# The mixer's two attentions as one pipeline of head pairs between projections

## The chip, the cores and the metric

The kernel runs on one core of a Trainium2 chip. The metric is device time of one execution in microseconds (us). The kernel before the change took 2604.03 us, the median of three runs (2603.2 to 2607.58).

## The reference, cut to what matters

Two transformer blocks follow each other on 256 tokens of width 1024, each two layers deep, all in float32. The change touches only the mixer sublayer of the first block, which runs twice (once in each layer):

```python
def mixer_sublayer(x, w_in, b_gate, kv_g, w_uk, w_uv, conv_w, w_branch, w_out, rel_bias):
    (qa, ckv, iq, ik, iw, qs, ks, vs, cb, cc, ch, ga, gb, gc) = jnp.split(x @ w_in, offsets, axis=-1)
    ckv = rms_norm(ckv, kv_g)
    y_a = dsa_branch(qa, ckv, iq, ik, iw, w_uk, w_uv, rel_bias)   # 8 heads, top-64 keys, softmax
    y_b = stick_breaking_branch(qs, ks, vs)                       # 8 heads of 64
    y_c = short_conv_branch(cb, cc, ch, conv_w)
    merged = (sigmoid(ga + b_gate[0]) * (y_a @ w_branch[0])
              + sigmoid(gb + b_gate[1]) * (y_b @ w_branch[1])
              + sigmoid(gc + b_gate[2]) * (y_c @ w_branch[2]))
    return merged @ w_out
```

`dsa_branch` scores all keys with eight index heads, keeps the best 64 of each query, and attends to a shared latent of width 128. `stick_breaking_branch` weighs key s by sig(z_ts) times the product of 1 - sig(z_tj) over the keys j between s and t.

## The kernel before, in words

Tokens lie in two blocks of 128. Every projection is a product of a weight and the activations, both split in two float32r parts, and takes three matmuls for each 128 rows of depth (`mm3`, L239 to L243). A projection of 2 x 128 output channels (`pair`, L252) is 48 such matmuls of 256 columns into one PSUM bank of the tag `pj`. Its weight comes in two halves of 512 KB through three buffers `wf` (SP issues the DMAs); ACT casts each half to `wh` (L236), DVE subtracts to get `wl` (L237). `wh` and `wl` have six buffers each. Everything else on TensorE, above all the attentions, uses plain float32 operands in the banks of the tag `pa`, four of them as well; a plain float32 matmul appears in the trace as two records.

The program is written in one order, but a scheduler arranges each engine's instructions within it, so projections written later are moved between the pieces of an attention.

In `mixer` the order as written is: the values `vs`; latent, index key and index weights; the index queries; eight index heads (L583 to L593: two score matmuls, a Relu on ACT, two accumulations on DVE each); the top-64 selection on DVE (L595 to L601); the projection `qa` (96 matmuls); the eight latent heads; the projections `qs` and `ks` (192); the eight stick heads; the short convolution (288); then for each of eight output blocks j its three gates (576 in all) and its branch product (36 each, 288 in all).

The heads run through `skew` (L209), a software pipeline: at step t the first stage works on unit t, the second on unit t - 1, and so on. A unit is one head. For the latent attention the stages are `logits` (every second head: the queries of a pair into the latent space, L626 and L627; a bias sum on GpSimd, L630 and L631; scores, L633 and L634; softmax), `turned` (three transposes, L316, copied out by ACT, L766), `latent` (L771, L772) and `values` (L656, into the left or right 64 columns of a bank). For the stick heads they are `sticks` (L675, L676, then sigmoids on ACT and scans on DVE), `turned` and `broken` (L771 and L772 with 64 output channels).

Side work is a generator queue: `fill(place)` advances it by the digits of the table `FILL` at the top of the file. In `logits` it takes three steps at the first three heads of each layer. Each step is a piece of the second block's modulation (L924: four matmuls on a tile `wa` of 512 KB, which has two buffers). `until(n)` (L229) forces the queue forward where its result is needed; the first place is the last feed-forward of the first block.

Of the kernel before, what the change touches and what calls it, by code (L numbers as in the profile page):

```python
# [13 lines left out]
AF = mybir.ActivationFunctionType  # L14
# [5 lines left out]
P = 128  # L20
# [94 lines left out]
class Net:  # L115
# [411 lines left out]
    def mixer(self, l, xs):  # L527
# [56 lines left out]
        for h in range(8):  # L584
            b = slice(64 * (h % 2), 64 * (h % 2) + 64)
            ps = self.ps()
            mm(ps[:, 0:P], iqT[b, h // 2, 0:P], ikT[b, 0:P], start=True, stop=True)
            mm(ps[:, P:384], iqT[b, h // 2, P:T], ikT[b, :], start=True, stop=True)
            re = self.a2()[:, :384]
            A.activation(re, ps[:, :384], AF.Relu)  # L590
            for tb, (a, e) in enumerate(G):
                prev = self.masks[:, 0, a:e] if h == 0 else sc[:, a:e]
                V.scalar_tensor_tensor(sc[:, a:e], re[:, a:e], iw[:, tb, h:h + 1], prev, ALU.mult, ALU.add)  # L593
# [22 lines left out]
        ys = [Split(self, 4) for _ in range(3)]  # L616
        qls, pos = {}, {}

        def logits(h, _):
            hp, i = divmod(h, 2)  # L620
            if i == 0:
                qls[hp] = self.a2().rearrange("p (c t) -> p c t", c=2)
                for j in range(2):
                    b = slice(64 * j, 64 * j + 64)
                    ps = self.ps()
                    mm(ps[:, :T], wuk[b, hp], qaT[b, hp], start=True, stop=True)  # L626
                    A.mul(qls[hp][:, j], ps[:, :T], 0.125)  # L627
            ql = qls[hp]
            bm = self.a2()[:, :384]
            nc.gpsimd.tensor_tensor(bm[:, P:384], t5[h // 4][:, h % 4, ::-1], sel[:, P:384], ALU.add)  # L630
            nc.gpsimd.tensor_tensor(bm[:, 0:P], t5[h // 4][:, h % 4, P - 1::-1], sel[:, 0:P], ALU.add)  # L631
            ps = self.ps()
            mm(ps[:, 0:P], ql[:, i, 0:P], ckT[:, 0:P], start=True, stop=True)  # L633
            mm(ps[:, P:384], ql[:, i, P:T], ckT, start=True, stop=True)  # L634
            V.tensor_tensor(bm, ps[:, :384], bm, ALU.add)
            p = self.a2()
            sm = self.softmax(bm, G, 1.0, p)
            self.scale_groups(p, G, sm)
            self.fill(f"logits{l}")
            return p  # L640

        def turned(h, p):
            return self.causalT(p)

        def latent(h, pT):
            ps = self.ps()
            self.causal_pv(ps[:, :T], [ckN[:, 0], ckN[:, 1]], pT)
            ol = self.a1()
            A.copy(ol, ps[:, :T])
            return ol  # L650

        def values(h, ol):
            hp, i = divmod(h, 2)
            if i == 0:
                pos[hp] = self.ps()
            mm(pos[hp][64 * i:64 * i + 64, :T], wuv[:, h], ol, start=True, stop=True)  # L656
            if i == 1:
                self.split(ys[0].h(hp), ys[0].l(hp), pos[hp][:, :T])

        self.skew([(h,) for h in range(8)], logits, turned, latent, values)  # L660


# [6 lines left out]
        pos = {}  # L669

# [22 lines left out]
        def broken(h, pT):  # L693
            hp, i = divmod(h, 2)
            if i == 0:
                pos[hp] = self.ps()
# [951 lines left out]
```

## Time and profile before

| | |
|---|---|
| median of the runs | 2604.03 us |
| the profiled execution | 2600.67 us |
| its span (first to last instruction) | 2598.8 us |
| TensorE busy | 2534.4 us (98%) |
| VectorE (DVE) busy | 1479.2 us (57%) |
| ScalarE (ACT) busy | 1175.3 us (45%) |
| GpSimd (POOL) busy | 66.7 us (3%) |
| read from HBM | 417.33 MB, 162 GB/s over the span |

Matmuls are pipelined: a row's duration is longer than the distance to the next row's start. What a matmul costs TensorE is therefore read from the difference of two starts. Idle time of an engine is told with what ended it.

### The profile page before, as it was taken

How to read it: one execution, taken by the hardware profiler on the slowest of the kernel's cores; microseconds unless marked ns; L12 is line 12 of the kernel's file. 1: busy time of each engine (PE TensorE's matmuls, PEld its weight loads, DVE VectorE, ACT ScalarE, POOL GpSimd, SP SyncE). 2: the span in 40 equal slices, each digit the busy share in tenths (PEclk: the TensorE clock that was granted, in tenths of full speed). 3: DMA queues.
4: the chain of work that ended last, by engine and by line, in shares of the span. 5: the costliest groups of instructions: out<-in, count | busy, mean ns of one | idle time of the engine just before them, and what ended most of it. 6: DMA issues, size and time to landing. Idle time of an engine off the chain costs nothing.

```text
span 2598.8 us, 40393 instructions
## 1 busy us (share of the span) xinstructions
PE 2534.4 (98%) x15946; PEld 2156.3 (83%) x15946; DVE 1479.2 (57%) x2974; ACT 1175.3 (45%) x1957; POOL 66.7 (3%) x88
## 2 busy tenths in 40 slices
PE   8999999999999999999999999899999999999999
PEld 7997889968988988799789877577888787777997
DVE  5556765556446547665665756776322337646644
ACT  5444454544444445544544545554222224445542
POOL 0000100000000000200000000000000000032000
PEclk9999999999999999999999999999999999999999
DMA  7565435655555555345665651434322434543553
GB/s 261 190 212 195 142 102 180 217 199 187 183 200 196 183 198 188 117 143 183 221 218 190 210 172 65 151 119 145 115 97 97 170 100 137 176 93 72 179 189 135
DMA packets 136493, 424.19 MB, mean 163 GB/s; under 512 B 29752, under 2 KB 32480, under 8 KB 136304
## 3 DMA queue, kind: packets, MB, share of 16 engines
q1 hardware_dynamic: 136304, 421.62, 49.3%
q8 instruction: 125, 2.05, 0.3%
q14 instruction: 64, 0.52, 0.1%
HBM read 417.33 MB, written 4.24 MB: 162 GB/s over the span
## 4 chain that ended last, share of the span: by engine, by line
PE 43%; DVE 3%; DMA 2%; ACT 1%; issue 1%; POOL 0%; SPq 0%; POOLq 0%; ACTq 0%; DVEq 0%
PE pj L241 8%; PE pj L242 8%; PE pj L243 8%; PE pa L242 4%; PE pa L241 4%; PE pa L243 4%; PE pa L316 2%; PE pj L924 1%; DMA wa<-in_mod_wB_dram 1%; DMA k<-in_rpbF_dram 1%; PE pj L1280 1%; DMA wf<-in_ffn_w_inA_dram 0%; PE pa L1295 0%; PE pj L1379 0%; PE pj L1243 0%
## 5 line engine op out<-in xcount | busy, mean ns | idle before, releaser
L237 DVE TENSOR_TENSOR wl<-wf,wh 128x1024 fp32r<-128x1024 f32 (+1 forms) x652 | 784.7, 1204 | 737.4 <-ACT wh L236 730.1
L236 ACT CAST wh<-wf 128x1024 fp32r<-128x1024 f32 (+1 forms) x652 | 670.7, 1032 | 930.8 <-PE pj L242 422.2
L241 PE MATMUL pj<-k,wh 128*128 128x256 f32 (+2 forms) x2896 | 840.6, 290 | 3.5 <-ACT k L236 3.5
L243 PE MATMUL pj<-k,wl 128*128 128x256 f32 (+2 forms) x2896 | 838.9, 290 | 0.0
L242 PE MATMUL pj<-k,wh 128*128 128x256 f32 (+2 forms) x2896 | 838.9, 290 | 0.0
L241 PEld LDWEIGHTS pj<-k,wh 128*128 128x128 f32 (+1 forms) x2896 | 554.2, 191 | 18.6 <-issue 6.6
L243 PEld LDWEIGHTS pj<-k,wl 128*128 128x128 f32 (+1 forms) x2896 | 554.1, 191 | 10.8 <-issue 3.4
L242 PEld LDWEIGHTS pj<-k,wh 128*128 128x128 f32 (+1 forms) x2896 | 554.0, 191 | 10.3 <-issue 3.2
L242 PE MATMUL pa<-wl,k 128*128 128x512 f32 x688 | 273.9, 398 | 0.0
L241 PE MATMUL pa<-wh,k 128*128 128x512 f32 x688 | 272.0, 395 | 0.0
L241 PE MATMUL pj<-wh,k 128*128 128x512 f32 (+1 forms) x616 | 246.9, 402 | 11.7 <-ACT wh L236 6.6
L242 PE MATMUL pj<-wl,k 128*128 128x512 f32 (+1 forms) x616 | 246.0, 400 | 0.0
L243 PE MATMUL pa<-wh,a 128*128 128x512 f32 x560 | 218.1, 389 | 0.0
L243 PE MATMUL pj<-wh,k 128*128 128x512 f32 (+1 forms) x496 | 197.4, 399 | 0.3 <-DVE k L237 0.3
L241 PEld LDWEIGHTS pa<-wh,k 128*128 128x128 f32 x688 | 128.8, 187 | 33.8 <-ACT wh L236 0.4
L241 PEld LDWEIGHTS pj<-wh,k 128*128 128x128 f32 x616 | 116.5, 189 | 48.3 <-issue 7.9
L242 PEld LDWEIGHTS pa<-wl,k 128*128 128x128 f32 x688 | 129.2, 188 | 28.4 <-issue 0.8
L242 PEld LDWEIGHTS pj<-wl,k 128*128 128x128 f32 x616 | 116.8, 190 | 29.7 <-DVE wl L237 2.3
L236 ACT CAST k<-k 128x512 fp32r<-128x512 f32 (+2 forms) x152 | 85.6, 578 | 104.2 <-PE pa L242 40.2
L243 PEld LDWEIGHTS pa<-wh,a 128*128 128x128 f32 x560 | 105.3, 188 | 25.3 <-issue 0.4
L243 PEld LDWEIGHTS pj<-wh,k 128*128 128x128 f32 x496 | 94.1, 190 | 23.3 <-DVE k L237 2.4
L316 PEld LDWEIGHTS pa<-ident,k 128*128 128x128 f32 x580 | 65.3, 143 | 50.3 <-issue 18.9
(254 smaller groups left out, 2461.7 us busy)
## 6 DMA issues: line engine op xcount, KB each, us to landing
wf<-in_ffn_w_inA_dram SPq DMA_DIRECT2D x262, 512.0 KB, 3.7
wf<-in_ffn_w_outB_dram SPq DMA_DIRECT2D x132, 512.0 KB, 3.9
wf<-in_mix_A_dram SPq DMA_DIRECT2D x108, 512.0 KB, 3.7
wa<-in_mod_wB_dram SPq DMA_DIRECT2D x96, 512.0 KB, 4.4
wf<-in_w_branchA_dram SPq DMA_DIRECT2D x32, 384.0 KB, 3.1
wf<-in_od_w_dram SPq DMA_DIRECT2D x24, 512.0 KB, 5.1
wf<-in_w_mix_outB_dram SPq DMA_DIRECT2D x16, 512.0 KB, 4.8
wf<-in_w_outB_dram SPq DMA_DIRECT2D x16, 512.0 KB, 7.9
```

The source lines that it names most:

```text
L236: self.nc.scalar.copy(h, x)
L237: self.nc.vector.tensor_tensor(l, x, h.bitcast(F32), ALU.subtract)
L241: mm(ps, sh, mh, start=start, stop=False)
L242: mm(ps, sh, ml, start=False, stop=False)
L243: mm(ps, sl, mh, start=False, stop=stop)
L316: self.nc.tensor.transpose(ps[:, i * P:(i + 1) * P], b, self.ident)
L924: mm(ps[32 * c:32 * c + 32, :256], self.cond[:, k], w[:, c * 256:c * 256 + 256], start=k == 0, stop=k == KT - 1)
L1280: mm(banks[i][:, j * T:(j + 1) * T], q["dqT"][b, h, c], k["dkT"][b, h], start=True, stop=True)
```

## The change: what it does

The two attentions become one `skew` over eight units (first four pairs of latent heads, then four pairs of stick heads) with the stages `queries`, `weights`, `turned`, `values` and `heads`. A new argument `step` calls `aside(t)` after the second stage of step t: one convolution block (72 projection matmuls) at steps 0 to 3, nothing at step 4, one pair of gates (48) at steps 5 to 11. The projections `qs` and `ks` stand ahead of the pipeline. The scores of the two heads of a pair lie in different 64 rows of the array and are issued in turn (`causal_scores`, used for the index heads too); the products with the values of a stick pair go to different 64 columns and are issued in turn (`causal_pv`); so are the two of `heads`. The calls `fill("logits...")` are gone. The branch loop makes only the gates that are still missing.

```diff
-    def skew(self, units, *stages):
+    def skew(self, units, *stages, step=None):
...
                     vals[t - n] = stage(*units[t - n], vals[t - n])
+                if n == 1 and step:
+                    step(t)
...
-        for h in range(8):
-            b = slice(64 * (h % 2), 64 * (h % 2) + 64)
-            ps = self.ps()
-            mm(ps[:, 0:P], iqT[b, h // 2, 0:P], ikT[b, 0:P], start=True, stop=True)
-            mm(ps[:, P:384], iqT[b, h // 2, P:T], ikT[b, :], start=True, stop=True)
...
+        for hp in range(4):
+            banks = self.causal_scores(iqT[:, hp], ikT)
...
-            self.fill(f"logits{l}")
...
-        self.skew([(h,) for h in range(8)], logits, turned, latent, values)
...
-        self.skew([(h,) for h in range(8)], sticks, turned, broken)
...
+        def queries(kind, hp, _):
+            if kind:
+                return None
+            ql = self.a2().rearrange("p (c t) -> p c t", c=2)
+            banks = [self.ps() for _ in range(2)]
+            for j in range(2):
+                b = slice(64 * j, 64 * j + 64)
+                mm(banks[j][:, :T], wuk[b, hp], qaT[b, hp], start=True, stop=True)
+            for j in range(2):
+                A.mul(ql[:, j], banks[j][:, :T], 0.125)
+            return ql
+
+        def weights(kind, hp, ql):
+            if kind:
+                banks = self.causal_scores(qsT[:, hp], ksT[:, hp])
+                return [sticks(ps) for ps in banks]
...
+        def turned(kind, hp, ps):
+            return [self.causalT(p) for p in ps]
+
+        def values(kind, hp, pTs):
+            ps = self.ps()
+            if kind:
...
+                self.causal_pv([ps[64 * i:64 * i + 64, :T] for i in range(2)], v, pTs)
+                self.split(ys[1].h(hp), ys[1].l(hp), ps[:, :T])
+                return None
+            for i in range(2):
+                self.causal_pv([ps[:, i * T:(i + 1) * T]], [[ckN[:, 0], ckN[:, 1]]], pTs[i:i + 1])
+            ol = self.a2().rearrange("p (c t) -> p c t", c=2)
+            A.copy(ol, ps.rearrange("p (c t) -> p c t", c=2))
+            return ol
+
+        def heads(kind, hp, ol):
+            if kind:
+                return
+            ps = self.ps()
+            for i in range(2):
+                mm(ps[64 * i:64 * i + 64, :T], wuv[:, 2 * hp + i], ol[:, i], start=True, stop=True)
+            self.split(ys[0].h(hp), ys[0].l(hp), ps[:, :T])
+
+        between = {0: (conv, 0), 1: (conv, 1), 2: (conv, 2), 3: (conv, 3)}
+
+        def aside(t):
+            if t in between:
+                between[t][0](*between[t][1:])
+            elif t > 4:
+                gate()
+
+        self.skew([(kind, hp) for kind in range(2) for hp in range(4)], queries, weights, turned, values, heads, step=aside)
...
             while len(gates) < 3 * j + 3:
...
+                gate()
...
+    def causal_scores(self, q, k):
...
+        banks = [self.ps() for _ in range(2)]
+        for qs, ks, cs in ((slice(0, P), slice(0, P), slice(0, P)), (slice(P, T), slice(0, T), slice(P, 384))):
+            for i in range(2):
+                b = slice(64 * i, 64 * i + 64)
+                mm(banks[i][:, cs], q[b, qs], k[b, ks], start=True, stop=True)
+        return banks
...
-    def causal_pv(self, ps, v, pT):
+    def causal_pv(self, pss, vs, pTs):
         mm = self.nc.tensor.matmul
-        mm(ps, v[0], pT[:, 0:T], start=True, stop=False)
-        mm(ps[:, P:T], v[1], pT[:, T:384], start=False, stop=True)
+        for ps, v, pT in zip(pss, vs, pTs):
+            mm(ps, v[0], pT[:, 0:T], start=True, stop=False)
+        for ps, v, pT in zip(pss, vs, pTs):
+            mm(ps[:, P:T], v[1], pT[:, T:384], start=False, stop=True)
```

Three places show what the scheduler makes of it on TensorE. In the rows, `pj` is a projection's bank and `pa` an attention's, `wh` and `wl` are the parts of a weight, `k` and `a` are activations and working tiles. The line numbers of the changed kernel differ: L243 to L245 are its three projection matmuls, L318 the transposes, L678 the queries, L694 and L695 the latent scores, L796 and L798 the products with the values, L739 the heads, L790 the stick scores, L950 the modulation.

The end of a latent pair, before: transposes and products of one head, and the two halves of `values` with the next pair's queries between them.

```order
L316 MATMUL pa_2993<-ident,a_520_2947 128x128
L771 MATMUL pa_2999<-a_525_2968,k_420_2489 128x256
L316 MATMUL pa_2993<-ident,a_520_2947 128x128 x2
L772 MATMUL pa_2999<-a_525_2968,k_420_2489 128x128
L656 MATMUL pa_3004<-a_527_2973,wuk_2739 64x256
L626 MATMUL pa_3007<-k_477_2741,wuk_2737 128x256
L626 MATMUL pa_3010<-k_477_2741,wuk_2737 128x256
L656 MATMUL pa_3004<-a_536_3002,wuk_2739 64x256
L241 MATMUL pj_3308<-k_330_2158,wh_3298 128x256
```

Now, after the last convolution block (step 4, where `aside` does nothing):

```order
L695 MATMUL pa_3724<-k_423_2498,a_606_3544 128x256
L318 MATMUL pa_3739<-ident,a_611_3558 128x128 x3
L318 MATMUL pa_3745<-ident,a_616_3576 128x128 x3
L796 MATMUL pa_3751<-a_631_3688,k_420_2489 128x256
L798 MATMUL pa_3751<-a_631_3688,k_420_2489 128x128
L796 MATMUL pa_3751<-a_633_3694,k_420_2489 128x256
L798 MATMUL pa_3751<-a_633_3694,k_420_2489 128x128
L243 MATMUL pj_3805<-k_330_2158,wh_3795 128x256
L739 MATMUL pa_3758<-a_635_3701,wuk_2739 64x256 x2
```

The six transposes of a pair stand together, and the two matmuls of `heads` follow each other; ahead of these rows stand the transposes and products of the pair before and the scores of the next pair, with no projection between them.

A stick pair, before: one head's transposes, products and scores.

```order
L316 MATMUL pa_3520<-ident,a_639_3487 128x128
L771 MATMUL pa_3526<-a_641_3499,k_368_2254 64x256
L316 MATMUL pa_3520<-ident,a_639_3487 128x128 x2
L772 MATMUL pa_3526<-a_641_3499,k_368_2254 64x128
L675 MATMUL pa_3529<-k_590_3171,k_589_3170 128x128
L676 MATMUL pa_3529<-k_590_3171,k_589_3170 128x256
L771 MATMUL pa_3526<-a_647_3524,k_368_2254 64x256
L772 MATMUL pa_3526<-a_647_3524,k_368_2254 64x128
L241 MATMUL pj_3691<-k_330_2158,wh_3632 128x256
```

Now, at the end of a gate pair's projection:

```order
L245 MATMUL pj_4040<-k_331_2159,wl_4037 128x256
L318 MATMUL pa_4092<-ident,a_680_3891 128x128 x3
L318 MATMUL pa_4098<-ident,a_683_3903 128x128 x3
L796 MATMUL pa_4104<-a_692_3978,k_368_2254 64x256
L796 MATMUL pa_4104<-a_694_3984,k_368_2254 64x256
L798 MATMUL pa_4104<-a_692_3978,k_368_2254 64x128
L798 MATMUL pa_4104<-a_694_3984,k_368_2254 64x128
L739 MATMUL pa_4113<-a_696_3991,wuk_2739 64x256 x2
L243 MATMUL pj_4160<-k_330_2158,wh_4150 128x256
```

The two heads of a pair now alternate in L796 and in L798.

The modulation's matmuls, before, at the start of the latent heads of the first layer:

```order
L626 MATMUL pa_2873<-k_477_2741,wuk_2737 128x256
L626 MATMUL pa_2876<-k_477_2741,wuk_2737 128x256
L924 MATMUL pj_2292<-wa_2336,cond_1054 32x256 x4
L924 MATMUL pj_2292<-wa_2901,cond_1054 32x256
L633 MATMUL pa_2882<-k_423_2498,a_498_2872 128x128
L634 MATMUL pa_2882<-k_423_2498,a_498_2872 128x256
L633 MATMUL pa_2906<-k_423_2498,a_498_2872 128x128
L634 MATMUL pa_2906<-k_423_2498,a_498_2872 128x256
L924 MATMUL pj_2292<-wa_2901,cond_1054 32x256 x3
L241 MATMUL pj_3184<-k_330_2158,wh_3174 128x256
```

Now there are none there; some of them stand in the second matrix of the last feed-forward of the first block, where `until(1)` calls for them:

```order
L245 MATMUL pa_15124<-wh_15127,a_2681_15138 128x512
L950 MATMUL pj_13774<-wa_15151,cond_1054 32x256 x4
L243 MATMUL pa_15123<-wh_15133,k_2680_15137 128x512
L244 MATMUL pa_15123<-wl_15134,k_2680_15137 128x512
L245 MATMUL pa_15123<-wh_15133,a_2681_15138 128x512
L243 MATMUL pa_15124<-wh_15133,k_2680_15137 128x512
L244 MATMUL pa_15124<-wl_15134,k_2680_15137 128x512
L950 MATMUL pj_13774<-wa_15157,cond_1054 32x256 x4
L245 MATMUL pa_15124<-wh_15133,a_2681_15138 128x512
```

Five tiles `wa` (19 matmuls as the program counts them) are used there within 35 projection matmuls of 512 columns.

## Rows read from the trace of the kernel before

**Rows 1.** The profile's page: span, and TensorE's busy time.

```profile
span 2598.8 us, 40393 instructions
...
PE 2534.4 (98%) x15946; PEld 2156.3 (83%) x15946; DVE 1479.2 (57%) x2974; ACT 1175.3 (45%) x1957; POOL 66.7 (3%) x88
```

**Rows 2.** Busy time by stage; columns are start:end, length, PE, PEld, DVE, ACT, POOL, clock, DMA.

```profile
269.09:370.20 101.11, 96.09 (x628) 76.95 (x628) 73.30 (x202) 50.66 (x115) 12.74 (x16) 0.97 0.30 103
370.20:496.10 125.90, 125.90 (x1050) 125.90 (x1051) 76.64 (x112) 62.49 (x89) 0.00 (x0) 1.00 0.58 185
1024.94:1124.30 99.36, 94.63 (x628) 76.39 (x628) 73.29 (x202) 50.45 (x115) 14.33 (x20) 0.98 0.34 112
```

**Rows 3.** Timeline of TensorE among projections: start, duration, engine, line, operation.

```profile
447.77 0.28 PE L243 MATMUL pj<-k,wl 128*128 128x256 f32 x1
447.89 0.28 PE L241 MATMUL pj<-k,wh 128*128 128x256 f32 x1
```

**Rows 4.** Groups of instructions on TensorE, 269.09 to 370.2 us (first layer's heads).

```profile
L241 PE MATMUL pj<-k,wh 128*128 128x256 f32 x135 | 40.0, 297 | 0.0
...
L316 PE MATMUL pa<-ident,a 128*128 128x128 f32 x48 | 10.9, 293 | 4.8 <-DVE a L506 4.2 <-DVE a L689 0.6
...
L924 PE MATMUL pj<-wa,cond 128*32 128x256 f32 x16 | 1.7, 390 | 0.0
```

**Rows 5.** Timeline of TensorE, the longest wait of that stage.

```profile
296.73 0.47 PE L316 MATMUL pa<-ident,a 128*128 128x128 f32 x1 [2.88 <-DVE a L506]
```

**Rows 6.** Busy time in the stretch from 296.65 us; the clock is the eighth column.

```profile
296.65:303.48 6.83, 6.75 (x22) 4.81 (x23) 3.27 (x9) 2.25 (x8) 1.25 (x2) 0.50 0.43 154
```

**Rows 7.** Timeline of TensorE through one latent pair.

```profile
312.20 0.42 PE L633 MATMUL pa<-k,a 128*128 128x128 f32 x2
...
312.89 0.49 PE L316 MATMUL pa<-ident,a 128*128 128x128 f32 x3
313.22 0.60 PE L771 MATMUL pa<-a,k 128*128 128x256 f32 x2
...
313.88 0.39 PE L633 MATMUL pa<-k,a 128*128 128x128 f32 x2
...
314.35 0.47 PE L243 MATMUL pj<-k,wl 128*128 128x256 f32 x1
314.65 0.28 PE L241 MATMUL pj<-k,wh 128*128 128x256 f32 x1
...
318.36 0.70 PE L626 MATMUL pa<-k,wuk 64*128 64x256 f32 x4
318.99 0.65 PE L656 MATMUL pa<-a,wuk 128*64 128x256 f32 x2
319.57 0.39 PE L242 MATMUL pj<-k,wh 128*128 128x256 f32 x1
```

**Rows 8.** Timeline of TensorE, stick heads: two heads' scores together, one head's products.

```profile
336.81 0.50 PE L675 MATMUL pa<-k,k 64*128 64x128 f32 x4
...
337.67 0.38 PE L241 MATMUL pj<-k,wh 128*128 128x256 f32 x1
...
354.36 0.65 PE L771 MATMUL pa<-a,k 128*64 128x256 f32 x2
...
355.15 0.39 PE L241 MATMUL pj<-k,wh 128*128 128x256 f32 x1
```

**Rows 9.** Timeline of TensorE in the second block: products of two heads in turn.

```profile
2326.78 1.09 PE L1408 MATMUL pa<-a,k 128*64 128x128 f32 x16
2327.80 0.49 PE L1379 MATMUL pj<-k,k 64*128 64x256 f32 x2
```

**Rows 10.** Groups of instructions on DVE, 400 to 490 us (first layer's branch products).

```profile
L237 DVE TENSOR_TENSOR wl<-wf,wh 128x768 fp32r<-128x768 f32 x14 | 13.4, 957 | 13.7 <-ACT wh L236 13.7
L753 DVE TENSOR_TENSOR k<-k,pj 128x256 f32<-128x256 f32 x21 | 8.2, 417 | 6.2 <-PE pj L243 6.2
```

**Rows 11.** The modulation's weight tiles over the whole span: from DMA issue to landing.

```profile
DMA to landing us min/median/max: 3.1/4.4/6.7
```

**Rows 12.** Groups of instructions on ACT, 269.09 to 370.2 us: what empties attention banks.

```profile
L766 ACT COPY a<-pa 128x384 f32<-128x384 f32 x16 | 7.5, 470 | 5.1 <-PE pa L316 5.0
...
L627 ACT ACTIVATE a<-pa 128x256 f32<-128x256 f32 x8 | 2.8, 386 | 0.4 <-PE pa L626 0.4
```

More of the change, by code (lines that the diff above doesn't have):

```diff
@@ L727, in mixer, with gate @@
             self.split(ys[2].h(t), ys[2].l(t), y)
-        bg = self.t([P, 3, KT], "bg", 1)
-        self.load(bg, I["b_gateT"][l])
-        gates = []
+        def gate():
+            ps = self.pair(wA[15 + len(gates) // 2], xs)
+            for c in range(2):
+                n = len(gates)
+                if n % 4 == 0:
+                    gate.g4 = self.four()
+                A.activation(gate.g4[:, n % 4], ps[:, c * T:(c + 1) * T], AF.Sigmoid, bias=bg[:, n % 3, n // 3:n // 3 + 1])
+                gates.append(gate.g4[:, n % 4])
@@ new lines, in probabilities @@
+        def probabilities(bm):
+            p = self.a2()
+            sm = self.softmax(bm, G, 1.0, p)
+            self.scale_groups(p, G, sm)
+            return p
+        def queries(kind, hp, _):
[9 more added lines that the diff above has]
+            return ql
@@ new lines, in weights @@
+        def weights(kind, hp, ql):
+            if kind:
+                banks = self.causal_scores(qsT[:, hp], ksT[:, hp])
+                return [sticks(ps) for ps in banks]
+            out = []
+            for i in range(2):
+                h = 2 * hp + i
+                bm = self.a2()[:, :384]
+                nc.gpsimd.tensor_tensor(bm[:, P:384], t5[h // 4][:, h % 4, ::-1], sel[:, P:384], ALU.add)
+                nc.gpsimd.tensor_tensor(bm[:, 0:P], t5[h // 4][:, h % 4, P - 1::-1], sel[:, 0:P], ALU.add)
+                ps = self.ps()
+                mm(ps[:, 0:P], ql[:, i, 0:P], ckT[:, 0:P], start=True, stop=True)
+                mm(ps[:, P:384], ql[:, i, P:T], ckT, start=True, stop=True)
+                V.tensor_tensor(bm, ps[:, :384], bm, ALU.add)
+                out.append(probabilities(bm))
+            return out
@@ new lines, in sticks @@
+        def sticks(ps):
+            z = self.a2()[:, :384]
+            V.tensor_tensor(z, ps[:, :384], self.masks[:, 2], ALU.add)
+            ns = self.a2()[:, :384]
+            A.activation(ns, z, AF.Sigmoid, scale=-0.125)
+            p = self.a2()
+            A.activation(p[:, :384], z, AF.Sigmoid, scale=0.125)
+            lt = z
+            for a, e in G:
+                V.memset(lt[:, e - 1:e], 1.0)
+                n = e - a
+                V.tensor_tensor_scan(lt[:, a:e - 1][:, ::-1], ns[:, e - 1:a:-1],
+                                     self.zero.broadcast_to((P, n - 1)), 1.0, ALU.mult, ALU.add)
+                V.tensor_tensor(p[:, a:e], p[:, a:e], lt[:, a:e], ALU.mult)
+            return p
@@ L735, in mixer @@
             while len(gates) < 3 * j + 3:
-                ps = self.pair(wA[15 + len(gates) // 2], xs)
-                for c in range(2):
-                    n = len(gates)
-                    if n % 4 == 0:
-                        g4 = self.four()
-                    A.activation(g4[:, n % 4], ps[:, c * T:(c + 1) * T], AF.Sigmoid, bias=bg[:, n % 3, n // 3:n // 3 + 1])
-                    gates.append(g4[:, n % 4])
+                gate()
             w = self.weight(I["w_branchA"][l, j], 1536)
```

94 lines of the change are left out of this document (19 added, 75 removed).

## The prediction

> **What bounds the kernel now.** I read the page first, then busy time by stage, then TensorE's timeline inside the stage that changes. TensorE is busy for 2534.4 of 2598.8 us [rows 1], so the reader is to see that no other engine can be the bound for long. A busy TensorE is not one at its peak, though, and the stages tell the two apart. While it projects, a matmul of 256 columns starts every 0.12 us [rows 3]; the stage after the heads, 1050 such matmuls in 125.9 us [rows 2], runs at exactly that rate, and nothing can be won there by moving work. The stage of the heads is different. In the first layer it takes 101.1 us [rows 2] and holds 403 projection matmuls (three groups, one of 135 and two of 134 [rows 4]), worth 48.4 us at 0.12, and 1.7 us of modulation [rows 4]. The other 51.0 us go to sixteen heads. In the second layer the same sum is 99.4 - 48.4 - 1.7 = 49.3 us [rows 2]. These 100.3 us in two layers are all that the change can shorten.
>
> They have three parts. Some is waiting: 4.8 us before transposes, for softmax on DVE [rows 4], 2.88 of it at once [rows 5]. Just then the granted clock stands at 0.50, the lower of its two levels (1.2 GHz), for 6.8 us [rows 6]. The rest is matmuls that leave half of the array unused, and the longer first matmul when projections resume.
>
> **The change part by part.** I price each pair of heads anew, by differences of starts, at full clock and with nothing to wait for.
>
> A latent pair: queries 318.99 - 318.36 = 0.63 us; scores of one head 312.89 - 312.20 = 0.69 and of the other 314.35 - 313.88 = 0.47; six transposes, twice 313.22 - 312.89 = 0.66; products with the latent, twice 313.88 - 313.22 = 1.32 [rows 7]. `heads` took 319.57 - 318.99 = 0.58 for each head [rows 7]. Now its two matmuls follow each other on different halves of the columns. What two halves in turn cost is shown in the second block: 16 records in 1.02 us, 64 ns each [rows 9], where a record of the same 128 columns of data in a full array costs 110 ns (three transposes in 0.33 us [rows 7]). So two cost 0.58 of what they cost singly, and `heads` of a pair costs 2 x 0.58 x 0.58 = 0.67. Returning to projections costs 0.30 instead of 0.12 for the first matmul (314.65 - 314.35) [rows 7], 0.36 for two returns in a pair. The sum is 0.63 + 1.16 + 0.66 + 1.32 + 0.67 + 0.36 = 4.80 us.
>
> A stick pair: scores of two heads on both halves of the rows 337.67 - 336.81 = 0.86 [rows 8]; transposes 0.66; products of one head 355.15 - 354.36 = 0.79 [rows 8], of two in turn 2 x 0.79 x 0.58 = 0.92; returns 0.36. The sum is 2.80 us.
>
> Four pairs of each make 30.4 us a layer. Against 51.0 and 49.3 that saves 20.6 + 18.9 = **39.5 us**, stalls and the low clock included. The products and `heads` rest on column halves whose overlap the mixer does not show. If they did not overlap, each layer would lose 4 x (0.66 + 0.49) = 4.6 us of it; if two cost no more than one, each would gain 4 x (0.13 + 0.09) = 0.9.
>
> On that row a rule can be weighed. The Trainium skill, TensorE: Matmul & The Clock Gate, Part 3 (Packing small matmuls), says that packed matmuls start about 4 ns apart and together last hardly longer than one. Rows 9 give a factor of 1.7, not 2. The sum goes by the row; by the rule it would be about 2 us shorter.
>
> Against this stand four new costs, the first three once a layer.
> - Queries and scores of a latent pair now stand back to back, with ACT's two scalings (0.39 us each [rows 12]) between them. I take 0.5 us of wait for each of four pairs, 2.0 us; bounds 0 and both scalings, 3.1.
> - At step 4 nothing is projected. Transposes, products, scores, transposes, products and `heads` take nine `pa` banks one after another where there are four, and the next scores need two more. A bank comes free when ACT copies it (0.47 us [rows 12]), but ACT first makes the exponentials that wait for DVE. I take 2.5 us, about the wait of rows 5; bounds 0 and twice that.
> - Fourteen gates are ready before the branch loop, so the first four output blocks have 36 projections, 4.32 us, against two weight halves (0.96 us each) and six small DVE operations (0.42 each) [rows 10], 4.43 us. DVE paces them by 0.1 us each; with a start I take 1.0, bounds 0 and 4.
> - The modulation's 16 records a layer leave the stage and cost the same 1.7 us elsewhere: no change, with cover or without. But five of their tiles are now wanted within 35 matmuls of 512 columns in the last feed-forward of the first block. A tile lands 4.4 us after its issue [rows 11], and only two buffers exist. I take 3 us once, bounds 0 and 10.
>
> The `qs` and `ks` projections move ahead of the heads, so the top-64 selection on DVE now has 288 + 72 projections, 43 us, beside it before anything on TensorE uses a softmax, so the wait of rows 5 should go. SP's queue gets the same loads in another order; the heads' stage uses 0.30 of the DMA engines [rows 2], so I cost the order at nothing.
>
> Sum: 39.5 - 2 x 5.5 - 3 = 25.5 us. Against the profiled execution, 2600.67 us, that gives 2575.2. The median of the runs is 3.4 us above it, so I predict **2579 us**, 1% less than before. About 0.2%, 5.2 us, is what a measurement of this kernel can tell from no change.
>
> **The rivals.**
> - *The new waits are hidden* (the scheduler finds projections for them): 39.5 us and up to 1.8 of fuller overlap are won, 2604.0 - 40 = 2564. For it: DVE and ACT are busy for 73.3 and 50.7 of 101.1 us [rows 2], so neither is full. Against it: step 4 has no projections of its own.
> - *Column halves do not overlap and the waits reach their upper bounds*: 39.5 - 9.2 - 2 x 12.1 - 10 leaves about -4; with half of that excess, 25.5 - 4.6 - 6.6 - 3.5 = 11 us, 2593. For it: rows 9 are of a narrower product, in another block.
> - *Slower: the four banks bound the pipeline.* If in every step TensorE waits for the round trip bank, ACT or DVE, copy, it pays at each of 16 pairs. It decides from 39.5 / 16 = 2.5 us per pair: a wait as long as the one of rows 5 at every pair, 2.88 us, costs 46 us and, with the 3 us of modulation, makes the kernel 10 us slower, 2614. For it: six to nine banks are taken per step. Against it: a copy takes 0.47 us, and a step holds 48 or 72 projections (5.8 or 8.6 us) in which four banks are emptied several times over. The Trainium skill, TensorEngine Tiling (Array Packing), PSUM Bottleneck, speaks for this rival: packing makes TensorE faster but not the emptying of PSUM. Rows 12 show ACT waiting for TensorE before those copies, not the other way.
> - *It does not do what it says*: the pieces were already woven between projections, 4.8 us of waiting was all there was, and new waits take as much. Then nothing can be measured, 2604.
>
> **How the numbers follow.** Forecast 0.60, hidden waits 0.16, weaker overlap 0.12, no change 0.06, slower 0.06. Faster by over 0.2%: 0.60 + 0.16 + 0.12 = 0.88; within 0.2%: 0.06; slower: 0.06. The low end is the hidden-wait case with its full bounds, 2561; the high end takes in the weaker overlap and a little more waiting, 2598. That leaves out the last two cases and the tails.
>
> **What would show it.** In the changed kernel's stage of the heads: four records of `heads` in about 0.67 us; four stick scores (eight records) in 0.86; the products of a stick pair in 0.92 or less; no long wait before the first latent transposes, and a granted clock of 1.00 from the first pair on. The new waits, if I am right about them, stand before the first stick scores (L790, released by ACT's copy) and before latent scores (L694, released by ACT's scaling), each under 3 us; the modulation's matmuls in the last feed-forward of the first block wait for their tiles. The time per layer from the first index score to the branch's end should fall by 12 to 16 us. I am wrong if TensorE's idle time in the mixer grows by more than 10 us a layer, or if records on different column halves start a full record apart.

## The result, and the profile after

The changed kernel took 2573.0 us, the median of four runs (2568.12 to 2580.95); the kernel before took 2603.61 us beside it. The ratio is 0.9882 (95% interval 0.9863 to 0.9900): 30.6 us faster, between 26 and 36. The prediction was 2579.0 us, in a range of 2561 to 2598, and faster at 0.88. The profiled execution is the longest of the four, 2580.95 us, so a second profile of the same kernel stands beside it below.

The profile's page of the changed kernel, span and busy time, answers to [rows 1]:

```profile
span 2579.1 us, 40360 instructions
...
PE 2514.6 (97%) x15946; PEld 2150.0 (83%) x15946; DVE 1477.5 (57%) x2974; ACT 1173.2 (45%) x1949; POOL 69.0 (3%) x88
```

Projections now stand among both attentions, so the stage of the heads [rows 2] has no counterpart of the same work. What can be compared is the whole mixer, from the first index score to the first matmul of the output projection. Busy time by stretch (start:end, length, PE, PEld, DVE, ACT, POOL, clock, DMA share, GB/s), before: the two mixers, and the stretch from the first score of the second cross attention to the second block's first latent expansion (L1142, later L1168; "the end of the first block" in the expectations).

```profile
265.13:496.13 231.00, 225.70 (x1709) 205.78 (x1709) 152.86 (x320) 117.14 (x211) 12.74 (x16) 0.99 0.47 153
1020.98:1249.45 228.47, 223.46 (x1706) 203.90 (x1705) 150.87 (x319) 115.11 (x209) 14.33 (x20) 0.99 0.48 154
1284.50:1565.72 281.22, 277.19 (x1773) 239.99 (x1774) 171.49 (x340) 136.78 (x214) 0.00 (x0) 1.00 0.59 197
```

The same three after:

```profile
267.22:478.71 211.49, 209.74 (x1693) 199.70 (x1693) 151.77 (x321) 114.80 (x207) 14.44 (x16) 1.00 0.50 161
1003.16:1213.29 210.13, 208.32 (x1681) 198.26 (x1681) 149.06 (x318) 112.56 (x204) 15.76 (x20) 1.00 0.50 161
1246.89:1540.61 293.72, 284.76 (x1830) 242.13 (x1830) 172.49 (x341) 137.80 (x215) 0.00 (x0) 0.99 0.60 200
```

The mixers are 19.5 and 18.3 us shorter, 37.8 in all. TensorE's idle time in them (length less busy) fell from 5.3 and 5.0 us to 1.75 and 1.8, and the granted clock is 1.00 throughout, where 6.8 us of the first mixer stood at 0.50 [rows 6]. The third stretch, in which no line was changed, became 12.5 us longer; it holds 57 more records. 56 of them are modulation: 16 and 24 records left the two mixers (1.68 and 2.25 us of TensorE's busy time there), and 16 more left the stretch between the second mixer and this one, because all steps come from one queue. This is where the gain was partly given back.

Three things announced for the timeline can be read in it. TensorE at step 4, where nothing is projected (start, duration, engine, line, operation; in brackets idle time and what ended it):

```profile
351.91 0.82 PE L318 MATMUL pa<-ident,a 128*128 128x128 f32 x6
353.59 0.70 PE L796 MATMUL pa<-a,k 128*128 128x256 f32 x2 [0.86 <-DVE a L696]
354.13 0.38 PE L798 MATMUL pa<-a,k 128*128 128x128 f32 x2
354.35 0.60 PE L796 MATMUL pa<-a,k 128*128 128x256 f32 x2
...
355.27 0.65 PE L739 MATMUL pa<-a,wuk 128*64 128x256 f32 x4
355.85 0.39 PE L244 MATMUL pj<-k,wh 128*128 128x256 f32 x1
```

The wait is there, but short: from 351.91 to 353.59 pass 1.68 us, where six transposes take 0.66 [rows 7]. The run below that fills the step prices all of it at 1.9. `heads` of a pair cost 355.85 - 355.27 = 0.58 us, what one head cost before [rows 7].

A wait before latent scores with ACT's operations around it, and a stick pair's transposes and products:

```profile
338.06 0.85 ACT L780 COPY a<-pa 128x384 f32<-128x384 f32 x2
338.59 0.49 PE L694 MATMUL pa<-k,a 128*128 128x128 f32 x2 [0.31 <-ACT a L780]
338.81 0.67 ACT L680 ACTIVATE a<-pa 128x256 f32<-128x256 f32 x2
...
392.36 0.82 PE L318 MATMUL pa<-ident,a 128*128 128x128 f32 x6
393.11 0.65 PE L796 MATMUL pa<-a,k 128*64 128x256 f32 x4
393.59 0.39 PE L798 MATMUL pa<-a,k 128*64 128x128 f32 x4
393.91 0.38 PE L243 MATMUL pj<-k,wh 128*128 128x256 f32 x1
```

Products of two heads take 393.91 - 393.11 = 0.80 us; one head alone took 0.79 [rows 8]. The wait before latent scores occurs once, 0.31 us, at one pair of four, and it ends with a copy that empties a bank of transposes (L780). The scaling of queries (L680) starts only when these scores have begun: it belongs to the next pair.

### The profile page after: what moved, and what is told of

It is laid out like the page before. It is cut to its first block, busy times and chain, and to the rows that moved or that the text cites. A ratio compares the mean times of both kernels' runs of the same rounds, so it can differ in the third digit from the quotient of the medians.

```text
span 2579.1 us, 40360 instructions
## 1 busy us (share of the span) xinstructions
PE 2514.6 (97%) x15946; PEld 2150.0 (83%) x15946; DVE 1477.5 (57%) x2974; ACT 1173.2 (45%) x1949; POOL 69.0 (3%) x88
## 4 chain that ended last, share of the span: by engine, by line
PE 82%; DVE 7%; DMA 5%; ACT 3%; issue 1%; SPq 0%; POOL 0%; ACTq 0%; DVEq 0%; POOLq 0%
PE pj L243 17%; PE pj L244 17%; PE pj L245 17%; PE pa L244 7%; PE pa L243 7%; PE pa L245 7%; PE pa L318 3%; PE pj L950 2%; DVE wl L239 2%; DMA wa<-in_mod_wB_dram 2%; DMA wf<-in_ffn_w_inA_dram 1%; ACT wh L238 1%; DMA wf<-in_mix_A_dram 1%; DVE mx L498 1%; PE pj L1306 1%
## 5 line engine op out<-in xcount | busy, mean ns | idle before, releaser
L239 DVE TENSOR_TENSOR wl<-wf,wh 128x1024 fp32r<-128x1024 f32 (+2 forms) x652 | 788.1, 1210 | 742.4 <-ACT wh L238 732.7
L238 ACT CAST wh<-wf 128x1024 fp32r<-128x1024 f32 (+2 forms) x652 | 670.4, 1032 | 934.4 <-PE pj L244 418.3
L243 PE MATMUL pj<-k,wh 128*128 128x256 f32 (+2 forms) x2896 | 840.6, 290 | 2.3 <-ACT k L238 2.3
L245 PE MATMUL pj<-k,wl 128*128 128x256 f32 (+2 forms) x2896 | 836.7, 289 | 0.0
L243 PEld LDWEIGHTS pj<-k,wh 128*128 128x128 f32 (+1 forms) x2896 | 553.7, 191 | 16.3 <-issue 5.7
L245 PEld LDWEIGHTS pj<-k,wl 128*128 128x128 f32 (+1 forms) x2896 | 553.8, 191 | 7.4 <-DVE k L239 0.4
L243 PE MATMUL pa<-wh,k 128*128 128x512 f32 x688 | 272.0, 395 | 0.0
L243 PE MATMUL pj<-wh,k 128*128 128x512 f32 (+1 forms) x616 | 247.4, 403 | 12.4 <-ACT wh L238 6.9
L245 PE MATMUL pa<-wh,a 128*128 128x512 f32 x560 | 218.3, 390 | 0.0
L245 PE MATMUL pj<-wh,k 128*128 128x512 f32 (+1 forms) x496 | 198.1, 400 | 0.5 <-DVE k L239 0.5
L243 PEld LDWEIGHTS pj<-wh,k 128*128 128x128 f32 x616 | 116.9, 190 | 49.3 <-ACT wh L238 7.8
L243 PEld LDWEIGHTS pa<-wh,k 128*128 128x128 f32 x688 | 128.8, 187 | 34.1 <-issue 1.0
L245 PEld LDWEIGHTS pa<-wh,a 128*128 128x128 f32 x560 | 105.3, 188 | 26.1 <-issue 1.2
L245 PEld LDWEIGHTS pj<-wh,k 128*128 128x128 f32 x496 | 94.2, 190 | 23.8 <-DVE k L239 3.3
L318 PEld LDWEIGHTS pa<-ident,k 128*128 128x128 f32 x580 | 66.1, 145 | 49.2 <-issue 18.9
```

The lines of the kernel that those rows point to most:

```text
L238: self.nc.scalar.copy(h, x)
L239: self.nc.vector.tensor_tensor(l, x, h.bitcast(F32), ALU.subtract)
L243: mm(ps, sh, mh, start=start, stop=False)
L245: mm(ps, sl, mh, start=False, stop=stop)
L318: self.nc.tensor.transpose(ps[:, i * P:(i + 1) * P], b, self.ident)
```

## The experiments

Each time is a median with the ratio to the kernel before, run beside it. Mixer lengths (first layer, second layer) are read as above.

**The changed kernel again.** No edit.

> The changed kernel once more, to tell its own scatter (2568.1 to 2580.9 in four runs) from the change. Theory: the profiled run lost some 8 us by chance, above all in the stretch from the second layer's cross attention to the end of the first block (293.7 us there against 281.2 before, with about 3.4 us of moved modulation and 3 us of waits for its tiles that belong to the change). Then a second profile shows that stretch at 285 to 290 us and a time near 2570. Rival: the stretch is 293 us again, and all of the 12.5 us is the price of the change.

2573.95 us, 0.9885 (0.9863 to 0.9906). The two mixers and the stretch up to the second block in its profile:

```profile
266.17:477.55 211.38, 209.72 (x1693) 199.67 (x1693) 151.64 (x321) 115.09 (x207) 14.36 (x16) 1.00 0.50 162
1000.75:1210.86 210.11, 208.29 (x1681) 198.25 (x1681) 148.83 (x318) 112.57 (x204) 15.85 (x20) 1.00 0.50 162
1244.45:1537.12 292.67, 284.25 (x1829) 241.85 (x1830) 172.36 (x341) 137.82 (x215) 0.00 (x0) 0.99 0.60 201
```

The mixers are the same to 0.1 as in the first profile. The stretch is 292.67 us, so the rival holds: its 11 to 12 us belong to the change. What did scatter is the last part of the kernel (from the end of that stretch on), 1038.5 us in the first profile and 1033.8 in the second. The mixers' 231.00 - 211.38 + 228.47 - 210.11 = 38.0 us is used from here on.

**One part alone: the stick queries and keys ahead, in the kernel before.**

```diff
+        qsT = self.four()
+        ksT = self.four()
+        for dst, u0 in ((qsT, 5), (ksT, 7)):
+            for u in range(2):
...
         self.skew([(h,) for h in range(8)], logits, turned, latent, values)
...
-        qsT = self.four()
-        ksT = self.four()
-        for dst, u0 in ((qsT, 5), (ksT, 7)):
-            for u in range(2):
...
```

> The kernel before with one part of the change: the projections of the stick queries and keys ahead of the latent heads. Theory: the stall before the first latent transposes goes, and with it the stretch at half clock: in each layer 2.9 us of waiting and 3.4 us of half speed, so the stage is 5 to 7 us shorter and the kernel 10 to 14 us faster than before, 2590 to 2594. Rival: the projections that are used up early are missing between the later heads, waits come up there, and the time stays within 3 us of before.

2592.94 us, 0.9958 (0.9943 to 0.9973): 10.8 us faster than its before, as the theory had it. Its two mixers:

```profile
266.49:490.69 224.20, 222.44 (x1710) 203.67 (x1709) 151.56 (x320) 117.00 (x211) 14.04 (x16) 1.00 0.48 157
1016.46:1239.48 223.02, 221.61 (x1706) 202.33 (x1705) 149.84 (x319) 115.22 (x209) 15.24 (x20) 1.00 0.48 158
```

They are 6.8 and 5.5 us shorter, and the clock is 1.00. The stall of [rows 5] and the half clock behind it were 12.3 of the 38.0 us, and to remove them it is enough to give the top-64 selection something to run beside.

**The pairs without the projections written between them.**

```diff
-        self.skew([(kind, hp) for kind in range(2) for hp in range(4)], queries, weights, turned, values, heads, step=aside)
+        self.skew([(kind, hp) for kind in range(2) for hp in range(4)], queries, weights, turned, values, heads)
+        for t in range(4):
+            conv(t)
```

> The changed kernel without the projections written between the steps: the convolution and all gates are written behind the pipeline, and the scheduler alone weaves them in. Theory: the pairs alone don't bring it; the scheduler puts smaller stretches of projections between the attention's pieces (the longest of 44 instead of 72 matmuls), waits come back, and the mixer's stage gets 3 to 8 us longer in each layer: 2580 to 2590. Rival: the scheduler's weaving is as good as the written one, and the time stays within 2 us of 2573.5.

2583.02 us, 0.9920 (0.9902 to 0.9938): 9 us slower than with them. Its mixers, 215.98 and 214.55 us:

```profile
266.83:482.81 215.98, 212.63 (x1693) 200.33 (x1693) 151.59 (x321) 115.14 (x206) 12.32 (x16) 1.00 0.49 158
1006.49:1221.04 214.55, 211.19 (x1682) 198.91 (x1682) 148.52 (x318) 112.92 (x203) 13.47 (x20) 1.00 0.49 159
```

TensorE idles 3.4 us in each (ACT's copies and scalings end most of it), against 1.7 and 1.8 with the written places; most of the rest of the 4.5 us a layer lies in the projections (24 returns to them instead of 18 in the first layer). Against the kernel with the projections ahead, the pairs as such shorten the mixers by 8.2 and 8.5 us, of which 3.9 in all are modulation that left. So, taken in this order, the 38.0 us are 12.3 for the projections moved ahead, 16.7 for pairs (with that modulation) and 9.0 for the places between the steps.

**Head after head within a pair.** In `causal_scores` and `causal_pv` the loop over the two heads becomes the outer one.

```diff
-        for qs, ks, cs in ((slice(0, P), slice(0, P), slice(0, P)), (slice(P, T), slice(0, T), slice(P, 384))):
-            for i in range(2):
-                b = slice(64 * i, 64 * i + 64)
+        for i in range(2):
+            b = slice(64 * i, 64 * i + 64)
+            for qs, ks, cs in ((slice(0, P), slice(0, P), slice(0, P)), (slice(P, T), slice(0, T), slice(P, 384))):
...
             mm(ps, v[0], pT[:, 0:T], start=True, stop=False)
-        for ps, v, pT in zip(pss, vs, pTs):
             mm(ps[:, P:T], v[1], pT[:, T:384], start=False, stop=True)
```

> The changed kernel with the matmuls of a pair issued head after head (scores of one head, then of the other; products likewise), pairs and places otherwise unchanged. Theory: scores gain nothing by taking turns (the eight index heads took 3.96 us head after head in the kernel before and 3.95 in turn in the changed one), the stick products do: a pair costs 0.80 us in turn, and 1.2 to 1.6 head after head. The mixer's stage gets 1.6 to 3.2 us longer in each layer, the time 3 to 6 us, to 2577 to 2580. Rival: TensorE overlaps neighbouring halves in either order, and the time stays within 1 us of the changed kernel's 2573.5.

2576.11 us, 0.9891 (0.9871 to 0.9911), the interval almost that of the changed kernel. The median is 2.2 us above that kernel's, but none of it lies in the mixers: they take 211.51 and 209.99 us, the same to 0.15. The theory fell. A stick pair's products in its timeline:

```profile
392.97 0.66 PE L796 MATMUL pa<-a,k 128*64 128x256 f32 x4
393.45 0.40 PE L798 MATMUL pa<-a,k 128*64 128x128 f32 x4
393.78 0.38 PE L243 MATMUL pj<-k,wh 128*128 128x256 f32 x1
```

0.81 us, although the first head's L798 now stands ahead of the second head's L796 in the program, in the scheduled order of TensorE's instructions too: all four records of L796 start before the first of L798. Taking turns, a large part of the diff's text, brings nothing that these runs can measure.

**Both heads on the same 64 columns.**

```diff
-                self.causal_pv([ps[64 * i:64 * i + 64, :T] for i in range(2)], v, pTs)
-                self.split(ys[1].h(hp), ys[1].l(hp), ps[:, :T])
+                [self.causal_pv([ps[0:64, i * T:i * T + T]], v[i:i + 1], pTs[i:i + 1]) for i in range(2)]
+                [self.split(ys[1].h(hp)[64 * i:64 * i + 64], ys[1].l(hp)[64 * i:64 * i + 64], ps[0:64, i * T:i * T + T]) for i in range(2)]
...
-                mm(ps[64 * i:64 * i + 64, :T], wuv[:, 2 * hp + i], ol[:, i], start=True, stop=True)
+                mm(ps[0:64, i * T:i * T + T], wuv[:, 2 * hp + i], ol[:, i], start=True, stop=True)
...
```

> The changed kernel with the two heads of a pair on the same 64 columns of the array (stick products and heads), each into its own part of the bank; two copies of half the width take the place of one. Theory: the two column halves run side by side in whatever order they are written (in turn or head after head both took 0.80 us for a stick pair, and one head alone took 0.79 in the kernel before), so without them a pair pays twice: 0.8 us more for the products and 0.5 to 0.6 for heads, four times each, 5 to 5.5 us a layer and 10 to 11 us in all, about 2584. Rival (what the pairs bring is fewer changes between projections and attention, not the halves): at most 3 us, 2576 or less.

2581.36 us, 0.9905 (0.9888 to 0.9922): 5 us slower by the ratios, 6.2 by the mixers (214.58 and 213.15 us), between theory and rival. A stick pair's products:

```profile
404.26 0.65 PE L796 MATMUL pa<-a,k 128*64 128x256 f32 x2
404.75 0.38 PE L798 MATMUL pa<-a,k 128*64 128x128 f32 x2
404.96 0.59 PE L796 MATMUL pa<-a,k 128*64 128x256 f32 x2
405.40 0.38 PE L798 MATMUL pa<-a,k 128*64 128x128 f32 x2
405.71 0.39 PE L243 MATMUL pj<-k,wh 128*128 128x256 f32 x1
```

1.45 us instead of 0.80, and `heads` took 0.96 to 1.01 instead of 0.53 to 0.58: 1.1 us a pair, 4.3 a layer. In the first layer the scheduler gave 1.1 us of it back (15 returns to projections instead of 18, scores in 7.9 us instead of 8.7). So the halves do run side by side and are worth about 6 of the 38 us, which is about half of what pairs bring beyond the modulation that left (16.7 - 3.9 = 12.8). The other half is not fewer returns to projections, nor shorter waits: the pairs alone, without the places, return 24 times in a layer, the kernel with the projections ahead 23 and 24 times, and TensorE idles 3.4 us a layer where it idled 1.8 and 1.4. What then makes it up was not tested by itself; the two heads' matmuls stand together, and with one half of the columns the products still take 11.1 us a layer, where the kernel with the projections ahead needs 12.8.

**A pair of gates at step 4.**

```diff
-            elif t > 4:
+            elif t >= 4:
```

> The changed kernel with a pair of gates at step 4 too, where nothing was projected. Theory: the waits of step 4 (0.9 us before the products of a pair, 1.0 us more around the transposes) go, 1.5 to 2.5 us a layer, so 3 to 5 us faster than the changed kernel, about 2569; no wait appears in the branch loop, which has one pair of gates less in its first blocks. Rival: the wait moves to another step or into the branch loop and the time stays within 2 us of the changed kernel.

2574.60 us, 0.9880 (0.9856 to 0.9904). The mixers are 209.52 and 208.07 us, 1.9 and 2.0 shorter than 211.38 and 210.11, as expected; in the total nothing is seen of these 3.9 us. Its stretch up to the second block was 295.7 us and its last part 1039.1, both long; whether that follows from the edit stays open.

**The modulation alone, taken out of the kernel before.**

```diff
-            self.fill(f"logits{l}")
+            pass
```

> The kernel before with the three modulation steps taken out of the latent heads, the one part of the change alone. Theory: the steps are done later at the same 3.4 us, the tiles crowd for about 3 us, and the stall before the first latent transposes loses little cover: 2 to 6 us slower than before, 2606 to 2610. Rival (crowding at the bound of 10 us or more): 2614 or more. Second rival: within 1 us of before.

2608.46 us, 1.0016 (1.0003 to 1.0029): 4.6 us slower than its before, between 1 and 8. The stretch up to the second block takes 290.7 us instead of 281.2; the parts ahead of it give back 4.5.

**The modulation put back, in the changed kernel.**

```diff
-                out.append(probabilities(bm))
+                out.append(probabilities(bm)); self.fill(f"logits{l}")
```

> The changed kernel with the three modulation steps put back into the first latent heads of each layer. Theory (the moved modulation costs what its waits for tiles show, 8.1 us of waiting over the kernel against 5.0 before): 2 to 5 us faster than the changed kernel, about 2569; the mixer's stage about 1.7 us longer in each layer, the stretch up to the end of the first block 6 us or more shorter. Rival (the whole 12.5 us that this stretch lost is the modulation): 9 to 13 us faster, about 2562. Second rival (the steps have cover anywhere): within 2 us of the changed kernel.

2564.62 us, 0.9845 (0.9823 to 0.9868): 9.3 us faster than the changed kernel, by the medians as much as the rival said. The stretch is short again, as the windows of this kernel show:

```profile
1252.51:1533.03 280.52, 277.07 (x1773) 239.99 (x1774) 171.29 (x340) 136.68 (x214) 0.00 (x0) 1.00 0.59 197
```

In the mixers the steps cost 0.7 and 1.2 us, less than the 1.7 and 2.2 of their records in the kernel before, since they cover waits: TensorE idles 0.9 us in each mixer now. From the first index score to the second block it is 5.7 us shorter than the changed kernel in its second profile; of the 9.3 the remainder lies in the last part, which scatters by more, so 9.3 is the looser of the two numbers. Where most of the loss sat is seen in the second cross attention. The changed kernel (second profile; L836 are its scores, L950 the modulation):

```profile
1254.07 0.59 PE L836 MATMUL pj<-k,k 128*128 128x256 f32 x2
1257.85 0.64 PE L950 MATMUL pj<-wa,cond 128*32 128x256 f32 x8 [3.19 <-DMA wa<-in_mod_wB_dram]
1259.07 1.06 PE L950 MATMUL pj<-wa,cond 128*32 128x256 f32 x2 [0.58 <-DMA wa<-in_mod_wB_dram]
1260.06 1.11 PE L318 MATMUL pa<-ident,a 128*128 128x128 f32 x4
```

Busy time of the same kernel right behind that wait:

```profile
1257.85:1261.20 3.35, 2.77 (x17) 1.15 (x20) 0.77 (x5) 0.00 (x0) 0.00 (x0) 0.63 0.76 271
```

With the modulation back in the heads, the same place:

```profile
1261.73 0.59 PE L836 MATMUL pj<-k,k 128*128 128x256 f32 x2
1262.25 0.63 PE L950 MATMUL pj<-wa,cond 128*32 128x256 f32 x6
1262.81 1.06 PE L980 MATMUL pj<-sel,k 128*128 128x8 f32 x8
1263.80 0.64 PE L950 MATMUL pj<-wa,cond 128*32 128x256 f32 x8
1264.39 1.68 PE L318 MATMUL pa<-ident,a 128*128 128x128 f32 x8
```

The steps form one queue, so leaving some out early shifts what every later place draws from it. The cross attention now draws 56 records in a row through two tile buffers; before it drew 48, with a step between them (L980) that needs no tile. TensorE stands at a tile for 3.8 us, with the cross attention's transposes queued behind it, and over the next 3.35 us its granted clock is 0.63 on average, between its two levels.

Of the 12.15 us by which the stretch differs in these two kernels, 6.9 have arisen when the last feed-forward starts, with 18 of the 56 records. The other 5.3 lie in that feed-forward: 38 records, and one more wait, for a normalized activation from DVE.

```profile
1451.25 1.06 PE L318 MATMUL pj<-ident,k 128*128 128x128 f32 x8 [1.93 <-DVE k L1021]
```

About half of the 12.15 us is the records' own time (17.95 us busy against 11.42), which other places no longer pay; the rest is waits and low clock.

**Both edits: modulation back, gates at step 4.**

> The changed kernel with both edits: modulation steps back in the first latent heads, and gates at step 4. Theory: the step-4 edit shortened the mixers by 1.9 and 2.1 us, which was lost in the crowded stretch of the second cross attention; with the modulation spread again it shows: 3 to 4 us faster than the kernel with the modulation steps alone (2564.6), 2560 to 2562. Rival: it is lost elsewhere again, 2564 to 2566.

2565.18 us, 0.9847 (0.9827 to 0.9867): the rival, 2564 to 2566. The mixers lose 1.6 us each against the kernel above, but the total shows none of it, for the second time.

**Fewer steps behind the second cross attention.**

```diff
-    "crossend1": "3",
+    "crossend1": "1",
```

> The changed kernel, modulation still out of the heads, with one step instead of three behind the second cross attention. Theory: what the moved modulation costs is the jam there (seven tiles in 21 us through two buffers, 3.2 us of waiting at once, and half clock behind it); with two tiles less the jam goes, and 3 to 6 us of the 9.3 come back: about 2569. Rival: the tiles only jam at the next place that calls for them, and the time stays within 2 us of 2573.5.

2586.46 us, 0.9917 (0.9903 to 0.9931), worse than either said. The wait in the cross attention stayed, 3.12 us, since the tiles were drawn ahead of the place that was cut, and the steps put off came due in the second block: the last part holds 64 more records of modulation and took 1046.2 us, 1033.8 before the edit.

**Five steps in the heads instead of three.** The edit that puts the modulation back, and in the table:

```diff
-    "logits0": "111", "logits1": "111",
+    "logits0": "11101010", "logits1": "11101010",
```

> The changed kernel with five modulation steps in the latent heads of each layer (after heads 1, 2, 3, 5 and 7) instead of three. Theory: the crowd in the second cross attention gets shorter still, its waits for tiles (0.7 us with three steps, 3.8 with none) stay away, and the records cost less than their 0.1 us each among the pairs: 1 to 4 us faster than with three steps (2564.6), 2561 to 2564. Rival: with the crowd gone the place of a step makes no difference: 2564 to 2566. Second rival: tiles and weights now compete in the mixer, waits for weights come up there: over 2567.

2584.50 us, 0.9914 (0.9899 to 0.9929), in the range of the second rival but not for its reason: the mixers are 213.81 and 212.11 us, and TensorE idles only 0.5 and 0.7 us in them. The shifted queue meets the cross attentions at a worse point. By the second block this kernel has also done 432 records of modulation, where the kernel with three steps has done 368, and its last part is no shorter for it (1033.3 us against 1031.1); so the run does not price the places alone. The second cross attention:

```profile
1273.04 0.64 PE L950 MATMUL pj<-wa,cond 128*32 128x256 f32 x8 [1.99 <-DMA wa<-in_mod_wB_dram]
...
1275.63 1.06 PE L950 MATMUL pj<-wa,cond 128*32 128x256 f32 x2 [0.91 <-DMA wa<-in_mod_wB_dram]
```

**Five steps in the heads, two instead of four in each cross attention.** As above, and:

```diff
-    "cross0": "1111", "cross1": "1111",
+    "cross0": "0101", "cross1": "0101",
```

> Five modulation steps in the latent heads of each layer and two in its cross attention, where the kernel with three in the heads has four; from the end of each cross attention on, the queue of steps stands where it stood in that kernel. Theory: what a step costs is decided by what stands around it; in the heads it has cover, in the cross attentions several tiles fall into some 20 us and the engine waits for them, and which step falls where is a matter of phase (so five steps alone cost 16 us). With the phase kept and two tiles less in each cross attention, their waits (0.6, 1.8 and 0.7 us in the first, 0.7 in the second) go: 1 to 4 us faster than with three steps (ratio to before 0.9845), a ratio of 0.983 to 0.984. Rival: the cross attentions need those steps as cover for their own waits for softmax, and the time is the same or up to 4 us longer, a ratio of 0.9845 to 0.986. Second rival: the phase in between (query projection of the cross attention) gets worse, 0.987 or more.

2574.26 us, 0.9889 (0.9871 to 0.9907): the second rival. The first cross attention still waits for a tile, now 3.3 us, and in the second the waits for softmax that the steps had covered come up (1.4 and 0.8 us before transposes). One of the waits that the theory counted for tiles, 1.8 us in the first cross attention, was for softmax in the kernel with three steps already. I know no rule for where the steps should stand; three in the heads, as before the change, was the best of the five distributions timed.

## Why the prediction was right, point by point

- **39.5 us gained in the heads' stage.** Right. The mixers became 38.0 us shorter; 3.9 of that is modulation that left, and the waits still in them come to 2 x 2.2 (below): 38.0 - 3.9 + 4.4 = 38.5. Its parts were less exact than the sum. Stick scores of a pair take 0.97 to 1.04 us among projections, not 0.86, and 1.70 at the first pair, whose heads stand apart; stick products 0.80, not 0.92; `heads` 0.53 to 0.58, not 0.67.
- **The factor 0.58 for column halves**, read from [rows 9], was the wrong one of the two weighed. The Trainium skill, TensorE: Matmul & The Clock Gate, Part 3 (Packing small matmuls), gives about 4 ns from start to start and hardly more than one matmul's time for both; here the two starts are 6 to 7 ns apart and two heads cost 0.80 us where one cost 0.79. With that the sum gains 4 x 0.2 us a layer, as the prediction's bound said.
- **That the halves overlap because they are issued in turn** was implied and is wrong: head after head they overlap as well.
- **Query to scores, 2.0 us a layer**: 0.3, and for another reason. The prediction read the two as back to back, but in `skew` the queries of a pair are made one step ahead of its scores, so its scaling has projections beside it; the 0.3 us is a wait for a bank. **Step 4, 2.5 us**: 1.9 and 2.0, by the kernel that fills it. **Branch loop, 1.0**: nothing; the 588 projections behind the last attention took 70.65 us, at 0.12 each 70.56. Together 2.2 instead of 5.5 a layer, 6.6 us less than was charged.
- **The signs announced.** The mixer was to become 12 to 16 us shorter in each layer and became 19.6 and 18.4 us shorter, 17.9 and 16.1 without the modulation that left: more than announced, by the waits charged too high. The longest new wait stands before products (L796, 0.86 us, ended by the DVE addition that empties a score bank, L696), not before stick or latent scores, where 0.2 and 0.3 us are seen.
- **Modulation, 3 us in the last feed-forward of the first block**: this is the step that failed, in place and size. It costs 4.6 us by the medians in the kernel before and 9.3 in the changed one (4.9 and 5.7 in the profiles up to the second block), and most of it sits in the second cross attention. In the last feed-forward the wait for a tile is 1.1 to 1.5 us, as it was before (1.4); new there is the wait for DVE, 1.4 and 1.9 us in the two profiles. I looked up where `until` calls for the moved steps and not what the shifted queue does at every place that draws from it.
- The two errors, 6.6 us too much for waits and 2 to 6 too little for modulation, partly cancel, and that is luck. The sum closes only roughly: 38.5 won, less 4.4 of waits and the 30.6 measured, leaves 3.5 us for modulation, less than either way of measuring it gives. The waits charged too high are the main reason that the gain was 30.6 us and not 25.5.
- **The slower rival**, four banks that bound every pair, did not occur: waits in the mixers fell to a third. Three short ones are still for banks: 0.86 us at step 4, 0.4 between the index scores, 0.3 before one pair's latent scores. The rival that the pieces were already woven is answered by the kernel left to the scheduler: pairs alone made the mixers 16.7 us shorter again than the moved projections had.

## What to carry to other kernels

A stall behind a slow selection costs more than its length where the clock falls after it, and moving independent projections ahead of it was a third of the gain for a few lines. When side work is drawn from one queue at fixed places, taking it out of one place moves it at all the later ones: read them all, above all those that are short of work themselves. The best of the thirteen kernels timed here are the two that keep the modulation steps where they were, at 0.9845 and 0.9847.

## What the hardware showed unexpectedly

Matmuls on different halves of the array's columns do not wait for each other in program order. In the kernel that issues a stick pair head after head, the second head's first record starts 13 ns after the first head's (392.972 and 392.985 us), and some 0.47 us before the first head's L798, which the program has ahead of it; at all eight stick pairs the two starts are 13 or 14 ns apart. The Trainium skill, TensorE: Matmul & The Clock Gate, Part 3 (Packing small matmuls), says that matmuls keep program order in their starts and ends; by the starts of this trace they do so only within a half, and the measurement decides (the ends in the profile are modelled, so nothing is said of those). The index scores of the kernel before, on different halves of the rows, show it too: written head after head, the first records of two heads start at 265.128 and 265.142 us, ahead of the first head's second matmul at 265.453. Eight heads took 3.96 us head after head and 3.95 in turn.
